# Output product of a hybrid layer: for two of four column groups, rows 8 to 11 move from plain products into the seven block products

## The chip, the cores and the metric

The kernel runs on one core of one Trainium2 chip. The metric is the device time of one execution in microseconds (us), median over runs; lower is better. The core's engines are PE (matrix products; PEld is its weight load), DVE (VectorE), ACT (ScalarE), POOL (GpSimd) and SP (SyncE, which only issues DMAs here).

## The reference

One layer on 512 tokens with 2048 channels. Only the last product is touched by the change.

```python
h = rms_norm(x, norm_g)
z = h @ w_in                                   # 2048 -> 7 x 1024
a_val, a_glu, a_gate, q, k, v, b_gate = split(z)
u = silu(layer_norm(causal_depthwise_conv(a_val * sigmoid(a_glu)), ...))
y_a = (u @ conv_pw_w + conv_pw_b) * silu(a_gate)                  # 1024
y_b = dilated_attention(rms(q), rms(k), v) * silu(b_gate)         # 1024, 16 heads
out = x + concat([y_a, y_b]) @ w_out                              # 2048 x 2048
```

## The kernel before, in words

**Number format.** Every large product is made of fp16 halves: an operand is scaled by a power of two and split into a high part (`A.activation(..., Copy, scale)`, on ACT) and a low part (`V.scalar_tensor_tensor(src, scale, hi, mult, subtract)`, on DVE). One product is then three matmuls (`tri`, L411: high by high L413, high by low L414, low by high L415). The scales come from bounds on the data: squares on ACT, a sum on PE, a reduction and a reciprocal on DVE, a shift and a masking on POOL (`bound`, L193).

**The output product.** The 2048 rows of `w_out` are 16 blocks of 128 rows. The left operand y has the same 16 blocks: 0 to 7 are mixer A ("a"), 8 to 11 are heads 0 to 7 of the attention ("b0"), 12 to 15 heads 8 to 15 ("b1"). The 2048 columns are four column groups g of 512, and the weights come in units of 4 blocks x 512 columns (1 MB; SP issues the load, `wf<-w_dram`). Each column group has

- a unit `("wb", g)`: rows 8 to 11, plain: 4 blocks x 4 token tiles x 3 = 48 matmuls of 128x512. After each token tile DVE adds the bank times a scale into the residual tile: `res<-ps_l,esc,res`, 128x512, four per unit. The scale `esc` is one tiny product on POOL (`evac_scale`, L421).
- three units `("wa", g)`: rows 12 to 15 and rows 0 to 7. Rows 0 to 7 are done as a 2x2 block product with seven products instead of eight (Winograd's form): p1, u, x, p7, p6, p5, z. For them both operands are cut in blocks (weights a11 ... a22, y b11 ... b22) and summed (weights s1 to s4, y t1 to t4). Weight sums s2, s3, s4 are accumulating DMAs that POOL issues (`wf<-wf`), s1 is a subtraction on DVE. Each part then has its high part on ACT and its low part on DVE (`ws<-wf,ws`, 128x1024). In groups 1 to 3 rows 12 to 15 join as a second, smaller set of seven ("c": weights `wsc`, 128x512); in group 0 they are plain, since their y is the last to be ready.

The y parts are `y<-...` on DVE (their low parts): 128x256 for a block, 128x512 for a plain row.

**The order of the work.** It is written out by hand. The program is a sequence of slots, each with 12 matmuls of 128x256 or 6 of 128x512, some 1.3 us. `after(n, fn)` puts a step n slots later, `calendar` by the slot's number. Every engine runs its own queue in program order and waits there for what it needs. The units of the four `wb` run while the last heads are still worked on, and `seven_parts(g)` and `seven_products(g)` give the slots of the weight parts and of the products in each `wa` group, `LENGTH` slots long. `b0` gets its scale `yb0` and its four splits after the fourth pair of heads; the scale `yab` of the other 12 blocks comes when the last head is done, and `y_parts` then makes one y split per slot. Tiles come from small pools: `wide` (8 tiles), `att` (4), `slots`, and `raw` (the fp32 weights), and a load or a split into a tile waits until its last reader is done.

Of the kernel before, what the change touches and what calls it, by code (L numbers as in the profile page):

```python
# [10 lines left out]
F32 = mybir.dt.float32  # L11
# [39 lines left out]
GROUPS += [(kind, g) for kind in ("wb", "wa") for g in range(4)]  # L51
# [34 lines left out]
def layer(ctx: ExitStack, tc: tile.TileContext, xt, w1, w2, w3, g_in, conv_w, conv_b,  # L86
# [156 lines left out]
    for kind, g in GROUPS:  # L243
        if kind == "pw":
            units += [(w2, g, p, kind, g) for p in range(8 // KU)]
        elif kind in OUT_K:
            units += [(w3, g, p, kind, g) for p in OUT_K[kind]]
        else:
            units += [(w1, IN_W1.index((kind, g)), p, kind, g) for p in range(KC // KU)]
# [365 lines left out]
    ob, ysum = {}, {}  # L615
# [6 lines left out]
    def put_y(part, i, y):  # L622

        whole, n, at = ("b0", 4, i) if part == "b0" else ("ab", 12, i + 8 * (part == "b1"))
        if whole not in ysum:
            ysum[whole] = small.tile([P, n], BF16, name=f"ysum{whole}", bufs=1)
        row_squares(y, ysum[whole][:, at:at + 1], S)
        yf[part][i] = y
        if part == "b0" and len(yf[part]) == n:
            def done(s, v):  # L630
                scales["yb0"] = (s, v)
                for k in range(n):
                    after(1 + 2 * k, lambda k=k: y16.update({k + 8: split16(yf["b0"].pop(k), s, "y16")}))
            after(2, lambda: bound("yb0", ysum[whole], done))
        elif part != "b0":
            if part == "a" and i >= 4:
                after(1, lambda: y_sums("", yf["a"], i - 4, i))
            if part == "b1" and i >= 2:
                after(1, lambda: y_sums("c", yf["b1"], i - 2, i))
            if len(yf["a"]) + len(yf["b1"]) == n:  # L640
                after(2, lambda: bound("yab", ysum[whole], y_parts, TOP - 1))
# [4 lines left out]
    def y_sums(c, y, k, below):  # L646

        b11, b12 = (y[k][:, f:f + H] for f in (0, H))
        b21, b22 = (y[below][:, f:f + H] for f in (0, H))
        t12, t34 = slot("ysum"), slot("ysum")  # L650
        t1, t2, t3, t4 = t12[:, :H], t12[:, H:], t34[:, :H], t34[:, H:]
        V.tensor_sub(t1, b11, b12)
        V.tensor_sub(t3, b12, b22)

        def rest():
            V.tensor_add(t2, b22, t1)
            V.tensor_sub(t4, b21, t2)

        after(1, rest)
        for name, t in (("b11", b11), ("b21", b21), ("b22", b22), ("t1", t1), ("t2", t2), ("t3", t3), ("t4", t4)):  # L660
            yt[name + c, k] = t

    def y_parts(s, v):

        scales["yab"] = (s, v)
        place = {}

        def block(name, k):
            with_ = {"b11": "t4", "b21": "t1", "t3": "t2", "t4c": "t3c", "t2c": "t1c"}.get(name)
            if name == "b22":  # L670
                if k % 2 == 0:
                    place["b22", k // 2] = slots.tile([P, 2, 2, H], F16, name="y16", tag="slot")
                t = place["b22", k // 2][:, k % 2]
            elif with_:
                place[with_, k] = slots.tile([P, 2, 2, H], F16, name="y16", tag="slot")
                t = place[with_, k][:, 0]
            else:
                t = place[name, k][:, 1]
            src = yt.pop((name, k))
            tparts[name, k] = (t[:, 0], t[:, 1])  # L680
            A.activation(t[:, 0], src, AF.Copy, scale=s)
            after(1, lambda: V.scalar_tensor_tensor(t[:, 1], src, s, t[:, 0], op0=OP.mult, op1=OP.subtract))

        def plain(k):
            t = slots.tile([P, 2, S], F16, name="y16", tag="slot")
            src = yf["b1"].pop(k)
            y16[12 + k] = (t[:, 0], t[:, 1])
            for b, f in ((1, 0), (2, H)):
                if k >= 2 or b == 1:
                    tparts[f"b{k // 2 + 1}{b}c", k % 2] = (t[:, 0, f:f + H], t[:, 1, f:f + H])  # L690
            A.activation(t[:, 0], src, AF.Copy, scale=s)
            after(1, lambda: V.scalar_tensor_tensor(t[:, 1], src, s, t[:, 0], op0=OP.mult, op1=OP.subtract))

        n = 1
# [155 lines left out]
    def fetch_res(j):  # L850

        if j < 6:
            res[j] = wide_tile("res", [P, 2, S], F32)
        else:
            res[j] = att.tile([P, 2, S], F32, name="res", tag="att")
        nc.sync.dma_start(res[j], rows_of(xt, j))
# [59 lines left out]
    LENGTH = (22, 21, 21, 21)  # L916
# [3 lines left out]
    wparts, plain_w, last, negative = {}, [], [], {}  # L920
    split = [set() for _ in range(4)]

    def seven_parts(g):
# [5 lines left out]
        def block(name):  # L929
            b = PLACE.get(name[:2] if name[0] == "s" else "", name[:3])  # L930
            t = raw[of[0]][:, 2 * (b[2] == "2"):][:, :2] if name[-1] == "c" else raw[of[1 if b[2] == "1" else 2]]
            return t[:, :, H * (b[1] == "2"):][:, :, :H]

        def add(name):

            c = name[2:]
            if name[:2] == "s1":
                V.tensor_tensor(block("a11" + c), block("a22" + c), block("a11" + c), op=OP.subtract)
            elif c and g == 2:
                x, to = SUMS[name[:2]]  # L940
                V.tensor_tensor(block(to + c), block(to + c), block(x + c), op=OP.add)
            else:
                x, to = SUMS[name[:2]]
                nc.gpsimd.dma_start(block(to + c), block(x + c), accum_op=OP.add)
# [3 lines left out]
        def hi(name):  # L948
            if name[-1] == "c":
                t = slots.tile([P, 2, 2, H], F16, name="wsc", tag="slot")  # L950
            else:
                t = part_pool.tile([P, 2, KU, H], F16, name="ws", tag="part")
            wparts[g, name] = t
            A.activation(t[:, 0], block(name), AF.Copy, scale=wscale["wa", g][0])  # L954

        def lo(name):
            t = wparts[g, name]
            V.scalar_tensor_tensor(t[:, 1], block(name), wscale["wa", g][0], t[:, 0], op0=OP.mult, op1=OP.subtract)
            done.add(name)
            if done >= {"s1", "s3"} and of[1] in raw:  # L960
# [3 lines left out]
            if done >= {"s1c", "s2c", "s3c", "s4c"}:  # L964
# [25 lines left out]
        for name, n in begin.items():  # L990
            for c, d in (("", 0), ("c", 1)) if g else (("", 0),):
# [4 lines left out]
    def both_scales(g):  # L996

        if g not in negative:
# [3 lines left out]
            negative[g] = e, ne  # L1002
        return negative[g]

    def seven_products(g):
# [12 lines left out]
        if g == 0:  # L1018
            banks_of.update(v=("22",), z=("12", ("s4", "b22")), u=("21", ("a22", "t4")), x=("11", ("a12", "b21")))
        else:  # L1020
            banks_of = {name: ((w, b), (w + "c", b + "c")) for name, ((w, b),) in banks_of.items()}
# [10 lines left out]
        def product(name, n, m):  # L1032

            what = banks_of[name][n]
            rows = 2 if what[0][-1] == "c" else KU
# [52 lines left out]
        if g == 0:  # L1088
            plan = [(2, alone), (4, lambda: into("22", "v")), (6, lambda: add("11", got["s"])), (12, lambda: into("21", "u")),
                    (14, lambda: (into("11", "x"), store("11"))), (16, lambda: into("22", "p5", ne)),  # L1090
                    (17, lambda: into("12", "p5")), (20, both)]
            order = (("p1", 0), ("v", 0), ("z", 0), ("u", 0), ("x", 0), ("u", 1), ("x", 1), ("p5", 0), ("p7", 0), ("p6", 0), ("z", 1))
            plan += [(2 * n + m, lambda name=name, k=k, m=m: product(name, k, m)) for n, (name, k) in enumerate(order)
                     for m in range(2)]
        else:
            plan = [(3, alone), (6, lambda: into("21", "u")), (7, lambda: add("11", got["s"])),
                    (9, lambda: (into("11", "x"), store("11"))), (15, both), (18, lambda: (into("22", "p5", ne), store("22"))),
                    (18, lambda: into("12", "p5"))]
            for n, name in enumerate(("p1", "u", "x", "p7", "p6", "p5", "z")):
                if (g, name) != (3, "z"):  # L1100
                    plan += [(3 * n + at, lambda name=name, k=k, m=m: product(name, k, m))
                             for at, k, m in ((0, 0, 0), (1, 0, 1), (2, 1, 0), (2, 1, 1))]
# [211 lines left out]

    for i in range(n_plain):
# [34 lines left out]
        else:  # L1350
# [14 lines left out]
            if i + 1 < len(units) and units[i + 1][3] == "wb":  # L1365
                for m in range(2):
                    extra[4 * m].append(lambda m=m: fetch_res(2 * units[i + 1][4] + m))
        if kind == "pw":
# [16 lines left out]
    for g in range(4):  # L1385
        plan = seven_parts(g) + [(n + LENGTH[g], fn) for n, fn in seven_parts(g + 1)] + seven_products(g)
        for n in range(LENGTH[g]):
            clock[0] = BEGIN[g] + n
            if n == 15 and g < 3:
# [55 lines left out]
```

## Time and profile before

| | |
|---|---|
| median of 3 runs | 815.13 us (815.05 to 815.55) |
| profiled execution | 815.08 us |
| its span in the trace | 813.3 us |
| instructions in the span | 13452 |

The span is the time between the first and the last instruction in the trace. The profile gives each engine's busy time and, in "waits", what ended each idle stretch of an engine that had work left. A row of the timeline has the start, the duration, the engine, the source line, the operation, output and inputs, partitions x elements, and in brackets the idle time just before with the instruction that ended it. A matmul's duration is longer than the distance from one to the next, since they are pipelined; the distance is what counts. The same holds, by 0.08 us, for DVE instructions that run back to back. The last units begin at these times of the span: `wb` 0 at 654.87 us, `wb` 2 at 677.51, `wa` 0 at 698.26, `wa` 1 at about 727.1.

### The profile page before, as it was taken

What the parts mean: (1) busy time and instruction counts of PE and PEld (TensorE: products, weight loads), DVE (VectorE), ACT (ScalarE), POOL (GpSimd) and SP (SyncE); (2) the same over time, 40 slices, a digit from 0 to 9 for tenths busy, and PEclk for the clock granted to TensorE, in tenths of its full rate; (3) what the DMA queues carried; (4) which work ended last, traced back from release to release, by engine and by line L of the source; (5) the groups of instructions that cost most, each with busy time, mean ns of one, the idle gap of its engine ahead of it and who ended that gap; (6) DMA issues with size and microseconds to landing.
All of it is one profiled execution on the core that took longest, in us unless ns stands there. A gap on an engine that the chain in (4) does not pass through costs nothing.

```text
span 813.3 us, 13452 instructions
## 1 busy us (share of the span) xinstructions
PE 806.7 (99%) x5271; PEld 500.9 (62%) x5271; DVE 703.3 (86%) x1188; ACT 557.5 (69%) x784; POOL 132.2 (16%) x143
## 2 busy tenths in 40 slices
PE   9999999999999999999999999999999999999998
PEld 6887745888646854444444444444444444788887
DVE  6768999878989989999999989997678798998885
ACT  6667687577756688586757658497688858766540
POOL 0001021322224300004012010000110002412420
PEclk9999999999999999999999999999999999999999
DMA  9852346983874863527474623526352487678752
GB/s 339 329 235 99 109 102 138 142 249 58 311 146 104 149 263 108 122 95 169 142 182 127 150 100 107 123 95 169 104 121 100 137 246 226 118 176 187 130 105 65
DMA packets 98367, 125.60 MB, mean 154 GB/s; under 512 B 62464, under 2 KB 83712, under 8 KB 89088
## 3 DMA queue, kind: packets, MB, share of 16 engines
q1 hardware_dynamic: 80544, 107.37, 42.2%
q0 software_dynamic: 17472, 17.30, 15.0%
q8 instruction: 41, 0.67, 0.3%
q14 instruction: 22, 0.18, 0.1%
q10 hardware_dynamic: 288, 0.07, 0.0%
HBM read 88.56 MB, written 4.19 MB: 114 GB/s over the span
## 4 chain that ended last, share of the span: by engine, by line
PE 90%; DVE 7%; ACT 1%; issue 1%; POOL 0%; DMA 0%; SPq 0%; ACTq 0%; DVEq 0%
PE ps_l L413 24%; PE ps_l L415 23%; PE ps_l L414 23%; PE ps_l L887 10%; DVE cv L81 3%; PE ps_s L413 2%; PE ps_s L415 2%; PE ps_s L414 2%; PE ps_s L730 2%; PE ps_o L771 2%; DVE wl L81 1%; DVE ws L81 1%; ACT junk L191 0%; DVE sx L81 0%; DMA x<-xt_dram 0%
## 5 line engine op out<-in xcount | busy, mean ns | idle before, releaser
L81 DVE SCALAR_TENSOR_TENSOR cv<-u,cw,cv 128x511 f32<-128x511 f32 (+14 forms) x240 | 162.1, 727 | 0.4 <-ACT cv L551 0.4
L191 ACT ACTIVATE junk<-wf 128x2048 uint8<-128x2048 f32 x68 | 129.1, 1899 | 2.4 <-DMA wf<-w_dram 2.1
L300 ACT ACTIVATE wh<-wf,ws 128x2048 f16<-128x2048 f32 x44 | 87.7, 1994 | 52.4 <-PE ps_l L414 50.6
L413 PE MATMUL ps_l<-x,wh 128*128 128x512 f16 x320 | 121.3, 379 | 0.3 <-DVE glu L81 0.3
L415 PE MATMUL ps_l<-x,wl 128*128 128x512 f16 x320 | 121.3, 379 | 0.0
L414 PE MATMUL ps_l<-x,wh 128*128 128x512 f16 x320 | 121.3, 379 | 0.0
L81 DVE SCALAR_TENSOR_TENSOR wl<-wf,ws,wh 128x2048 f16<-128x2048 f32 x45 | 105.6, 2346 | 10.7 <-ACT wh L300 10.7
L413 PE MATMUL ps_l<-wh,x 128*128 128x512 f16 x256 | 97.1, 379 | 0.0
L415 PE MATMUL ps_l<-wh,x 128*128 128x512 f16 x256 | 97.0, 379 | 0.0
L414 PE MATMUL ps_l<-wl,x 128*128 128x512 f16 x256 | 97.0, 379 | 0.0
L81 DVE SCALAR_TENSOR_TENSOR ws<-wf,ws 128x1024 f16<-128x1024 f32 x70 | 89.0, 1278 | 7.1 <-ACT ws L1138 4.5
L413 PEld LDWEIGHTS <-wh 128*128 128x128 f16 x480 | 47.0, 98 | 55.3 <-issue 4.0
L415 PEld LDWEIGHTS <-wl 128*128 128x128 f16 x480 | 46.9, 98 | 53.6 <-DVE wl L81 0.4
L414 PEld LDWEIGHTS <-wh 128*128 128x128 f16 x480 | 46.9, 98 | 50.4 <-issue 0.7
L887 PE MATMUL ps_l<-xr,wr 128*128 128x512 f32 x288 | 69.6, 397 | 0.7 <-ACT xr L338 0.7
L205 POOL TENSOR_SCALAR ws<-ws 128x1 f32<-128x1 f32 x22 | 11.8, 537 | 324.4 <-DVE ws L81 295.6
L887 PEld LDWEIGHTS ps_l<-xr,wr 128*128 128x128 f32 x288 | 53.8, 188 | 14.3 <-ACT xr L338 1.5
L413 PEld LDWEIGHTS <-x 128*128 128x128 f16 x352 | 34.4, 98 | 32.5 <-issue 1.9
L415 PEld LDWEIGHTS <-x 128*128 128x128 f16 x352 | 34.4, 98 | 31.3
L414 PEld LDWEIGHTS <-x 128*128 128x128 f16 x352 | 34.4, 98 | 30.1
L954 ACT ACTIVATE ws<-wf,ws 128x1024 f16<-128x1024 f32 x28 | 32.1, 1147 | 28.3 <-PE ps_l L415 9.7
L1138 ACT ACTIVATE ws<-wf,ws 128x1024 f16<-128x1024 f32 x42 | 47.1, 1138 | 5.8 <-PE ps_l L415 4.8
(251 smaller groups left out, 1816.3 us busy)
## 6 DMA issues: line engine op xcount, KB each, us to landing
wf<-w_dram SPq DMA_DIRECT2D x72, 1024.0 KB, 5.2
wf<-wf POOLq DMA_DIRECT2D x30, 512.0 KB, 6.5
x<-xt_dram SPq DMA_DIRECT2D x16, 256.0 KB, 6.7
res<-xt_dram SPq DMA_DIRECT2D x8, 512.0 KB, 6.6
out_dram<-res SPq DMA_DIRECT2D x15, 256.0 KB, 2.2
wf<-w_dram SPq DMA_DIRECT2D x7, 512.0 KB, 7.2
wf<-wf POOLq DMA_DIRECT2D x6, 256.0 KB, 6.3
wf<-w_dram SPq DMA_DIRECT2D x2, 256.0 KB, 3.1
```

Source lines behind the costliest of these rows:

```text
L81: return getattr(self.engine, name)(out, src, *args, **kw)
L191: A.activation(junk[:, :n], src, AF.Square, scale=scale, accum_out=acc)
L205: G.tensor_scalar(scale, scale, 1e-30, 2.0 ** (-2 * top), op0=OP.max, op1=OP.mult)
L300: A.activation(parts[i][0], raw[i], AF.Copy, scale=wscale[units[i][3:]][0])
L413: T.matmul(ps, ah, bh, start=first, stop=False, skip_group_check=more)
L414: T.matmul(ps, ah, bl, start=False, stop=False, skip_group_check=more)
L415: T.matmul(ps, al, bh, start=False, stop=last, skip_group_check=more)
L730: T.matmul(ps[i, a], qk["q", hf][p4 // 2][rows, p4 % 2, q, i * P:w], qk["k", hf][p4 // 2][rows, p4 % 2, k, :w], start=n == 0, stop=n == 2)
L771: T.matmul(po[rows, i * P:(i + 1) * P], vs[hf][j // 2][:, j % 2, 2 * p4 + a, vp * DH:(vp + 1) * DH], got["t", a][:, pp * (ALL // P) + FROM ...
L887: T.matmul(banks[group, m], wt[:, a, m * P:(m + 1) * P], xk[b], start=k == 0 and a == b == 0, stop=k == KC - 1 and a == 1)
L954: A.activation(t[:, 0], block(name), AF.Copy, scale=wscale["wa", g][0])
L1138: A.activation(t[:, 0], block(name, pair), AF.Copy, scale=wscale[group][0])
```

## The change

For groups g in `JOINED = (0, 1)` the unit `wb` is gone. Its rows 8 to 11 join the seven products as a third set "d": each of the seven products gets 12 more matmuls of 128x256 into a bank that is open anyway (84 per group instead of 48 of 128x512), and four DVE additions per group fall away. For them

- the y of rows 8 to 11 gets block sums (8 additions) and 8 t parts "t1d" to "t4d" (`b0_parts`, in the `pw` units, with the four plain splits that stood behind the fourth pair of heads);
- each joined group gets seven weight parts "d" (`wsd`, 128x512, high on ACT and low on DVE), one more subtraction (s1d) on DVE, three more accumulating DMAs on POOL (s2d, s3d, s4d, 256 KB each) and a scale `wjs` (two tiny products on POOL);
- `y_parts` issues its splits four in three slots, `1 + n * 3 // 4`, instead of one per slot;
- the residual tiles of groups 0 and 1 are fetched later, and the plans of both groups are written anew (`LENGTH` 29 and 28 slots instead of 22 and 21).

```diff
+JOINED = (0, 1)
+GROUPS += [("wb", g) for g in range(4) if g not in JOINED] + [("wa", g) for g in range(4)]
...
+            units += [(w3, g, p, kind, g) for p in OUT_K[kind] + (2,) * (kind == "wa" and g in JOINED)]
...
-            def done(s, v):
-                scales["yb0"] = (s, v)
-                for k in range(n):
-                    after(1 + 2 * k, lambda k=k: y16.update({k + 8: split16(yf["b0"].pop(k), s, "y16")}))
-            after(2, lambda: bound("yb0", ysum[whole], done))
+            after(2, lambda: bound("yb0", ysum[0][:, :4], lambda s, v: scales.update(yb0=(s, v)), TOP - 1))
...
+    def b0_parts():
+        y = yf["b0"]
+        s = scales["yb0"][0]
+        for k in range(4):
+            after(2 * k, lambda k=k: plain("b0", k, s))
+        for k in range(2):
+            after(6 + 3 * k, lambda k=k: y_sums("d", y, k, k + 2))
+            for n in range(4):
+                after(21 + 2 * (2 * n + k), lambda name=f"t{n + 1}d", k=k: block(name, k, s))
...
     def y_parts(s, v):
         scales["yab"] = (s, v)
+        both_scales(0)
+        n = 0
         for name in ("b11", None, "t4", "b21", "t1", "t3", "t2", "b22", "t4c", "t3c", "t2c", "t1c"):
             for k in range(2 if name and name[-1] == "c" else 4):
-                after(n, lambda name=name, k=k: block(name, k) if name else plain(k))
+                after(1 + n * 3 // 4, lambda name=name, k=k: block(name, k, s) if name else plain("b1", k, s))
                 n += 1
...
-    LENGTH = (22, 21, 21, 21)
+    LENGTH = [29, 28, 21, 21]
...
+            elif name[-1] == "d":
+                near = (g, name) in ((0, "a11d"), (0, "a22d"))
+                t = (wide if near else att).tile([P, 2, 2, H], F16, name="wsd", tag="wide" if near else "att")
...
         if g == 0:
-            adds = [(3, "s1", add), (4, "s4", add), (-2, "s2", add), (-8, "s3", add)]
-            begin = {"a11": -6, "a22": -4, "a12": 0, "s1": 5, "s3": 8, "s2": 12, "s4": 16}
+            adds = [(-8, "s3", add), (-2, "s2", add), (3, "s1", add), (4, "s4", add),
+                    (-7, "s3d", add), (5, "s2d", add), (10, "s1d", add), (13, "s4d", add)]
+            begin = {"a11": -6, "a11d": -4, "a22": -3, "a22d": 4, "a12": 0, "s1": 6, "a12d": 11, "s3": 12, "s1d": 14, "s2": 15,
+                     "s3d": 18, "s4": 20, "s2d": 21, "s4d": 24}
...
+            if g in JOINED:
+                t = joined_scale[g] = small.tile([P, 1], F32, name="wjs", bufs=2)
+                G.tensor_tensor(t, wscale["wa", g][0], scales["yab"][0], op=OP.mult)
+                G.tensor_tensor(t, t, scales["yb0"][1], op=OP.mult)
...
+            for name, k in (("p1", 0), ("p1", 1), ("v", 0), ("z", 0), ("u", 0), ("x", 0), ("u", 1), ("u", 2), ("x", 1), ("x", 2),
+                            ("p5", 0), ("p5", 1), ("p7", 0), ("p7", 1), ("p6", 0), ("p6", 1), ("z", 1), ("z", 2)):
...
+    calendar.setdefault(8 * of_group["pw", 0][0] + 6, []).append(b0_parts)
```

Three queues show how the work moves. First POOL, from the scale `yab` on (`yabs`): `esc<-wi,yabi` is the scale of group 0, `nesc` its negative, `esc<-wi,yb0i` that of a `wb` unit, and the DMAs are the accumulations s3, s3d and s2 of group 0. In the kernel before:

```order
L205 TENSOR_SCALAR yabs<-yabs 128x1
L169 TENSOR_TENSOR yabs<-yabs,half 128x1
L426 TENSOR_TENSOR esc<-wi,yb0i 128x1
L205 TENSOR_SCALAR ws<-ws 128x1
L169 TENSOR_TENSOR ws<-ws,half 128x1
L426 TENSOR_TENSOR esc<-wi,yb0i 128x1
L944 DMA wf<-wf 128x4x256
L426 TENSOR_TENSOR esc<-wi,yb0i 128x1
L944 DMA wf<-wf 128x4x256
L426 TENSOR_TENSOR esc<-wi,yabi 128x1
L1001 TENSOR_SCALAR nesc<-esc 128x1
```

and in the changed one:

```order
L206 TENSOR_SCALAR yabs<-yabs 128x1
L170 TENSOR_TENSOR yabs<-yabs,half 128x1
L427 TENSOR_TENSOR esc<-wi,yabi 128x1
L1031 TENSOR_SCALAR nesc<-esc 128x1
L1035 TENSOR_TENSOR wjs<-ws,yabs 128x1
L1036 TENSOR_TENSOR wjs<-wjs,yb0i 128x1
L960 DMA wf<-wf 128x4x256
L960 DMA wf<-wf 128x2x256
L427 TENSOR_TENSOR esc<-wi,yb0i 128x1
L960 DMA wf<-wf 128x4x256
```

The last `esc` of a `wb` unit (unit 3) now stands behind the scales of group 0 and two DMAs, all of which stand behind `yabs`.

Second DVE, from the reciprocal of `yab` on. `res` is the addition of a finished bank, `wl` the low part of a plain weight unit, `y_...<-ag` and `y_...<-ysum` low parts of y blocks, `y_...<-gate` of 128x512 those of plain rows. Before:

```order
L81 RECIPROCAL yabi<-yabs 128x1
L81 SCALAR_TENSOR_TENSOR res<-ps_l,esc,res 128x512
L81 SCALAR_TENSOR_TENSOR y_6749<-ag_5132,yabs,y_6749 128x256
L81 SCALAR_TENSOR_TENSOR wl<-wf,ws,wh 128x2048
L81 SCALAR_TENSOR_TENSOR y_6760<-ag_5132,yabs,y_6760 128x256
L81 SCALAR_TENSOR_TENSOR res<-ps_l,esc,res 128x512
L81 SCALAR_TENSOR_TENSOR y_6774<-ag_5173,yabs,y_6774 128x256
L81 SCALAR_TENSOR_TENSOR y_6784<-ag_5173,yabs,y_6784 128x256
```

and after the change:

```order
L82 RECIPROCAL yabi<-yabs 128x1
L82 SCALAR_TENSOR_TENSOR y_6512<-ysum,yb0s,y_6512 128x256
L82 SCALAR_TENSOR_TENSOR res<-ps_l,esc,res 128x512
L82 SCALAR_TENSOR_TENSOR y_6540<-ysum,yb0s,y_6540 128x256
L82 SCALAR_TENSOR_TENSOR y_6765<-ag_5125,yabs,y_6765 128x256
L82 SCALAR_TENSOR_TENSOR y_6767<-ag_5125,yabs,y_6767 128x256
L82 SCALAR_TENSOR_TENSOR wl<-wf,ws,wh 128x2048
L82 SCALAR_TENSOR_TENSOR y_6779<-ag_5165,yabs,y_6779 128x256
L82 SCALAR_TENSOR_TENSOR ws<-wf,ws 128x1024
L82 SCALAR_TENSOR_TENSOR res<-ps_l,esc,res 128x512
L82 SCALAR_TENSOR_TENSOR y_6797<-ag_5165,yabs,y_6797 128x256
```

The addition `res` that follows the reciprocal belonged to unit `wb` 1 of four; it is now the first of unit 3, the last plain one, and the first weight part `ws` of group 0 (a11) stands eight instructions behind the reciprocal instead of 34.

Third DVE again, within the work of group 0, in the changed kernel alone (`wsd` is new): `wsd` is the low part of a joined weight part, here a22d, and `wf<-wf` the subtraction s1.

```order
L82 TENSOR_TENSOR wf<-wf 128x4x256
L82 SCALAR_TENSOR_TENSOR y_6917<-gate,yabs,y_6917 128x256
L82 SCALAR_TENSOR_TENSOR y_6941<-gate,yabs,y_6941 128x256
L82 SCALAR_TENSOR_TENSOR wsd<-wf,wjs,wsd 128x512
L82 SCALAR_TENSOR_TENSOR res<-ps_l,esc,res 128x2x256
L82 SCALAR_TENSOR_TENSOR y_6900<-ysum,yabs,y_6900 128x256
```

These stand in one queue with the y splits, and all of them come between the reciprocal and the last products of group 0.

More of the change, by code (lines that the diff above doesn't have):

```diff
@@ L639, in put_y @@
                 after(1, lambda: y_sums("c", yf["b1"], i - 2, i))
-            if len(yf["a"]) + len(yf["b1"]) == n:
-                after(2, lambda: bound("yab", ysum[whole], y_parts, TOP - 1))
+            if len(yf["a"]) + len(yf["b1"]) == 12:
+                after(2, lambda: bound("yab", ysum[0], y_parts, TOP - 1))
     yt, tparts = {}, {}
@@ L660, in y_sums, with block @@
         for name, t in (("b11", b11), ("b21", b21), ("b22", b22), ("t1", t1), ("t2", t2), ("t3", t3), ("t4", t4)):
-            yt[name + c, k] = t
+            if name[0] == "t" or not c:
+                yt[name + c, k] = t
+    place = {}
+    def block(name, k, s):
+        with_ = {"b11": "t4", "b21": "t1", "t3": "t2", "t4c": "t3c", "t2c": "t1c"}.get(name)
+        if name == "b22":
+            if k % 2 == 0:
+                place["b22", k // 2] = slots.tile([P, 2, 2, H], F16, name="y16", tag="slot")
+            t = place["b22", k // 2][:, k % 2]
+        elif name[-1] == "d":
+            if ("d", k) not in place:
+                place["d", k] = att.tile([P, 4, 2, H], F16, name="y16", tag="att")
+            t = place["d", k][:, int(name[1]) - 1]
+        elif with_:
+            place[with_, k] = slots.tile([P, 2, 2, H], F16, name="y16", tag="slot")
+            t = place[with_, k][:, 0]
+        else:
+            t = place[name, k][:, 1]
+        src = yt.pop((name, k))
+        tparts[name, k] = (t[:, 0], t[:, 1])
+        A.activation(t[:, 0], src, AF.Copy, scale=s)
+        after(1, lambda: V.scalar_tensor_tensor(t[:, 1], src, s, t[:, 0], op0=OP.mult, op1=OP.subtract))
@@ new lines, in plain @@
+    def plain(part, k, s):
+        t = slots.tile([P, 2, S], F16, name="y16", tag="slot")
+        src = yf[part][k]
+        if part == "b1":
+            yf[part].pop(k)
+        c, at = ("c", 12) if part == "b1" else ("d", 8)
+        y16[at + k] = (t[:, 0], t[:, 1])
+        for b, f in ((1, 0), (2, H)):
+            if k >= 2 or b == 1:
+                tparts[f"b{k // 2 + 1}{b}{c}", k % 2] = (t[:, 0, f:f + H], t[:, 1, f:f + H])
+        A.activation(t[:, 0], src, AF.Copy, scale=s)
+        after(1, lambda: V.scalar_tensor_tensor(t[:, 1], src, s, t[:, 0], op0=OP.mult, op1=OP.subtract))
@@ L684, in plain @@
[L684 to L692, printed above, removed]
@@ L850, in fetch_res @@
     def fetch_res(j):
[L852 to L855, printed above, removed]
+        res[j] = wide_tile("res", [P, 2, S], F32)
         nc.sync.dma_start(res[j], rows_of(xt, j))
@@ L953, in hi, with scale_of @@
             wparts[g, name] = t
-            A.activation(t[:, 0], block(name), AF.Copy, scale=wscale["wa", g][0])
+            A.activation(t[:, 0], block(name), AF.Copy, scale=scale_of(name))
+        def scale_of(name):
+            return joined_scale[g] if name[-1] == "d" else wscale["wa", g][0]
         def lo(name):
             t = wparts[g, name]
-            V.scalar_tensor_tensor(t[:, 1], block(name), wscale["wa", g][0], t[:, 0], op0=OP.mult, op1=OP.subtract)
+            V.scalar_tensor_tensor(t[:, 1], block(name), scale_of(name), t[:, 0], op0=OP.mult, op1=OP.subtract)
             done.add(name)
+            if done >= {"s1d", "s2d", "s3d", "s4d"} and g in JOINED and of[3] in raw:
+                free(of[3])
             if done >= {"s1", "s3"} and of[1] in raw:
@@ L1034, in product @@
             what = banks_of[name][n]
-            rows = 2 if what[0][-1] == "c" else KU
+            rows = 2 if what[0][-1] in "cd" else KU
             for to, tokens in spot(name, m):
@@ new lines, in seven_products @@
+            n = 0
+            for name, k in (("p1", 0), ("p1", 1), ("v", 0), ("z", 0), ("u", 0), ("x", 0), ("u", 1), ("u", 2), ("x", 1), ("x", 2),
+                            ("p5", 0), ("p5", 1), ("p7", 0), ("p7", 1), ("p6", 0), ("p6", 1), ("z", 1), ("z", 2)):
+                joined = banks_of[name][k][0][-1] == "d"
+                plan += [(n + m * (not joined), lambda name=name, k=k, m=m: product(name, k, m)) for m in range(2)]
+                n += 1 if joined else 2
+        else:
+            w = LENGTH[g] // 7
+            plan = [(w, alone), (2 * w, lambda: into("21", "u")), (2 * w + 1, lambda: add("11", got["s"])),
+                    (3 * w, lambda: (into("11", "x"), store("11"))), (5 * w, both),
+                    (6 * w, lambda: (into("22", "p5", ne), store("22"))), (6 * w, lambda: into("12", "p5"))]
```

76 lines of the change are left out of this document (33 added, 43 removed).

## The prediction

> **What bounds the kernel now.** I read the page first: busy shares, the slices, the chain that ended last.
>
> ```profile
> PE 806.7 (99%) x5271; PEld 500.9 (62%) x5271; DVE 703.3 (86%) x1188; ACT 557.5 (69%) x784; POOL 132.2 (16%) x143
> PEclk9999999999999999999999999999999999999999
> ```
>
> PE is busy 99% of the span of 813.3 us, at full clock in every slice. Whatever shortens PE's work shortens the kernel, as long as the others keep up. DVE, at 86%, has the least room of them. Next the waits of PE, all of which come to 3 us; two matter here:
>
> ```profile
> PE ps_s L147 <- POOL wz L144: 1.0, 1, 1.0
> PE ps_s L575 <- DVE lnacc L81: 1.0, 1, 1.0
> ```
>
> Then the windows around the change. Columns: PE busy, PEld, DVE, ACT, POOL (instructions), granted clock, DMA share, GB/s.
>
> ```profile
> 623.80:634.10 10.30, 10.30 (x49) 4.67 (x48) 10.13 (x26) 9.93 (x19) 0.00 (x0) 1.00 0.47 155
> 634.10:644.50 10.40, 10.40 (x50) 4.70 (x49) 6.47 (x11) 10.40 (x22) 0.00 (x0) 1.00 0.17 54
> 644.50:654.90 10.40, 10.40 (x51) 4.73 (x50) 9.07 (x18) 5.09 (x7) 1.08 (x4) 1.00 1.02 250
> 654.90:669.20 14.30, 14.30 (x120) 7.29 (x119) 13.79 (x28) 8.37 (x13) 0.94 (x3) 1.00 0.70 234
> 669.20:698.30 29.10, 29.10 (x138) 13.17 (x136) 25.49 (x39) 22.63 (x35) 4.84 (x5) 1.00 0.68 217
> 698.30:727.10 28.80, 28.80 (x266) 25.81 (x265) 25.76 (x44) 21.46 (x32) 11.77 (x12) 1.00 0.69 148
> ```
>
> The first four are the `pw` units and the first plain output units, the fifth the rest of the plain units, the sixth group 0 of the block products. In the last two PE never stops, and DVE works 51.3 of 57.9 us. So PE is the bound, and DVE's queue is 11% away from it in the very stretch to which the change adds DVE work. That is what the forecast turns on.
>
> **What the change takes from PE.** The distance between matmuls, from the first and last of 78 of 128x512 and of 94 of 128x256:
>
> ```profile
> 499.86 0.38 PE L413 MATMUL ps_l<-x,wh 128*128 128x512 f16 x1
> ...
> 516.48 0.38 PE L415 MATMUL ps_l<-x,wl 128*128 128x512 f16 x1
> 716.73 0.27 PE L414 MATMUL ps_l<-y,ws 128*128 128x256 f16 x1
> ...
> 726.89 0.27 PE L414 MATMUL ps_s<-y,ws 128*128 128x256 f16 x1
> ```
>
> 16.62 us / 77 = 0.2158 us and 10.16 / 93 = 0.1092 us. A joined group loses 48 x 0.2158 = 10.36 us and gets 84 x 0.1092 = 9.17, a gain of 1.18; two groups give 2.4 us. The new matmuls have the shape and the alternation of weights of the second row pair, so I put no bounds on this.
>
> Four low parts of 128x512 leave DVE's queue from ahead of `lnacc`, at 0.66 us each (rows below) 2.6 us. PE's wait of 1.0 us there should go. Bounds 0, should DVE be late there for something else, and 1.0; I take 1.0. ACT, at 69%, gets 22 small instructions more, and SP two issues; I cost both at nothing, because in the fifth and sixth windows ACT is idle for 13.8 of 57.9 us.
>
> **What it adds to DVE.** The distances of DVE's instructions, with `wl` 128x2048, `ws` 128x1024, `res` and y 128x512, y 128x256, and the forms whose mean is all I have (less 0.08 us of overlap):
>
> ```profile
> 691.81 2.35 DVE L81 SCALAR_TENSOR_TENSOR wl<-wf,ws,wh 128x2048 f16<-128x2048 f32 x1
> 694.07 0.48 DVE L81 SCALAR_TENSOR_TENSOR y<-ysum,yabs,y 128x256 f16<-128x256 f32 x1
> 694.47 1.28 DVE L81 SCALAR_TENSOR_TENSOR ws<-wf,ws 128x1024 f16<-128x1024 f32 x1
> 695.66 0.74 DVE L81 SCALAR_TENSOR_TENSOR res<-ps_l,esc,res 128x512 f32<-128x512 f32 x1
> 696.32 0.87 DVE L81 SCALAR_TENSOR_TENSOR y<-ysum,yabs,y 128x256 f16<-128x256 f32 x2
> 697.11 1.28 DVE L81 SCALAR_TENSOR_TENSOR ws<-wf,ws 128x1024 f16<-128x1024 f32 x1
> 678.38 0.74 DVE L81 SCALAR_TENSOR_TENSOR y<-gate,yabs,y 128x512 f16<-128x512 f32 x1
> 679.04 0.16 DVE L81 TENSOR_REDUCE ws<-ps_s 128x1 f32<-128x3 f32 x1
> L81 DVE SCALAR_TENSOR_TENSOR wsc<-wf,ws,wsc 128x512 f16<-128x512 f32 x21 | 15.6, 743 | 0.0
> L81 DVE TENSOR_TENSOR wf<-wf 128x1024 f32<-128x1024 f32 x10 | 12.2, 1217 | 1.1 <-DMA wf<-wf 1.1
> ```
>
> That is 2.26, 1.20, 0.66, 0.66 and 0.40 us; `wsd` has the form of `wsc`, 0.66; the subtraction 1.14.
>
> Nothing of y blocks 0 to 7 can be split before the scale `yab`, and all of it must be split for the products. So I add up one queue, from the reciprocal of `yab` to the low part of s2d, the weights of the second half of product p6 of group 0. In the changed program 70 DVE instructions stand in between: 37 y of 256 (14.8 us), 7 `ws` (8.4), 6 `wsd` (4.0), 9 `res` (5.9), 4 y of 512 (2.6), one `wl` (2.3), the subtractions s1 (1.1) and s1d (0.6, half the size), a `res` addition (0.6) and three tiny ones (0.2): 40.5 us.
>
> What PE has to do meanwhile: before the products of s2d come 300 matmuls of group 0, 300 x 0.1092 = 32.8 us, and the rest of the plain units ahead. Those two units and the attention pair between them take, from the first to the third unit's start, 677.51 - 654.87 = 22.64 us, as in the trace:
>
> ```profile
> 654.87 0.38 PE L413 MATMUL ps_l<-y,wh 128*128 128x512 f16 x1
> ...
> 677.51 0.38 PE L413 MATMUL ps_l<-y,wh 128*128 128x512 f16 x1
> 669.13 0.17 DVE L81 RECIPROCAL yabi<-yabs 128x1 f32<-128x1 f32 x1
> ```
>
> The reciprocal ended 14.4 us after the first of those starts. At that distance 8.2 us of plain work are left behind it, instead of 698.26 - 669.30 = 29.0 before. The second plain pair is what used to hide the y splits, and its removal is the heart of the loss. The reciprocal also comes later: ahead of it DVE gets 4 y of 512, 8 additions and 6 t parts of 256, 4 x 0.66 + 14 x 0.40, about 8 us. In the first four windows DVE was idle for 45.4 - 39.5 = 5.9 us, so about 2 us stick out. Bounds: nothing (idle time further ahead takes them) and 3.9 (half of them, since idle time lies where something else is awaited). Taken 2.0: PE has 6.2 + 32.8 = 39.0 us of work (bounds 8.2 - 3.9 + 32.8 = 37.1 and 8.2 + 32.8 = 41.0), against DVE's 40.5.
>
> **New waits in that queue.** DVE's second instruction after the reciprocal is the first `res` of plain unit 3, which needs its `esc` from POOL. That now stands behind group 0's `esc`, `nesc`, two `wjs` and two DMAs, all released by the reciprocal. The POOL rows:
>
> ```profile
> 680.56 0.19 POOL L426 TENSOR_TENSOR esc<-wi,yb0i 128x1 f32<-128x1 f32 x1
> 680.73 1.35 POOL L944 DMA_DIRECT2D wf<-wf  x1
> 681.62 2.61 POOL L426 TENSOR_TENSOR esc<-wi,yb0i 128x1 f32<-128x1 f32 x1
> 700.42 2.95 POOL L1001 TENSOR_SCALAR nesc<-esc 128x1 f32<-128x1 f32 x1
> 704.88 3.87 POOL L944 DMA_DIRECT2D wf<-wf  x3 [1.50 <-DMA wf<-wf]
> ```
>
> At the least 4 x 0.19 + 2 x 0.9 (from a DMA's start to the next instruction's) + 0.19 = 2.7 us; at the most 0.19 x 3 + 2.95 + 2 x 1.3 + 0.3 = 6.4. DVE gets there after 0.4, so it waits 2.3 to 6.0 us. I take 4.6: the nearest row is the `esc` behind a DMA, which took 2.61 us instead of 0.19, and here it stands behind two (2.7 - 0.19 + 2.61 - 0.4 = 4.7). Behind the waiting `res` stand all y splits and the first weight part, a11, without which p1 cannot begin: PE's gap shows first there.
>
> The Trainium skill ("SBUF — State Buffer", A bandwidth-pool intuition that's wrong) says that a DMA issued on GpSimd which takes about 620 ns alone takes about 3100 ns beside a VectorE instruction that holds their shared port, since the descriptors can't be written. The slow `esc` row fits that. By that rule DVE's own waiting would free the port, and the wait would be at its lower end: a sum lower by 2.3 us, 817.9.
>
> Two subtractions, s1 and s1d, change the raw weights in place and wait for accumulating DMAs that read them, and those DMAs wait for low parts just ahead in DVE's own queue. Landing times, and the wait of this kind now:
>
> ```profile
> wf<-wf POOLq DMA_DIRECT2D x30, 512.0 KB, 6.5
> wf<-wf POOLq DMA_DIRECT2D x6, 256.0 KB, 6.3
> DVE wf L81 <- DMA wf<-wf: 1.1, 1, 1.1
> ```
>
> 5.1 and 5.3 us of DVE work lie between, so 1.4 and 1.0 are missing: 2.4 us. Bounds: 0, if DVE by then is late for other reasons, and 3.9, with the 1.50 us that the last POOL row waited for its predecessor's data.
>
> Group 1 I cost at nothing. Its window before:
>
> ```profile
> 727.10:754.60 27.50, 27.50 (x254) 24.65 (x252) 24.21 (x32) 18.01 (x21) 7.49 (x8) 1.00 0.80 164
> ```
>
> DVE's 24.2 us get 7 `wsd` and an s1d, 5.2, against 28 slots x 12 x 0.1092 = 36.7 us of PE: 7 us of cover. Were it gone, the same two waits as in group 0 would come again, 2.4 us (in rival 4).
>
> **The sum.** Stall of PE = 40.5 + 4.6 + 2.4 - 39.0 = 8.5 us. Low: 40.5 + 2.3 + 0 - 41.0 = 1.8. High: 40.5 + 6.0 + 3.9 - 37.1 = 13.3. The profiled execution, 815.08, has 1.8 us around its span and stands at the median of 815.13, so I count from 815.1: 815.1 - 2.4 - 1.0 + 8.5 = 820.2 us.
>
> **The rivals.** 0.2% (1.6 us: 813.5 to 816.8) is about what a measurement of this kernel can tell from no change.
>
> 1. *Faster: DVE keeps up.* The one mechanism: the reciprocal comes no later and DVE's waits on POOL and DMA stay at their low ends. Speaking for it: the 5.9 idle us would nearly take the added 8, and POOL is busy 16%. Against it: POOL cannot run ahead, since its row starts with the same scale. It decides at a stall of 1.8 us, just at the low bound: 811.7 to 813.5 us.
> 2. *No change.* A stall of 1.8 to 5.1 us, with one wait of the two at its low end: 813.5 to 816.8; around 815 the 3.4 us of gain are just eaten.
> 3. *A colder PE on top.* The first matmuls of the span, after idle time, go at another pace:
>
> ```profile
> L147 PE MATMUL ps_s<-wz 128*128 128x512 f16 x9 | 3.4, 557 | 1.0 <-POOL wz L144 1.0
> ```
>
> Nine took 3.44 us instead of 8 x 0.2158 + 0.38 = 2.1, so a restart costs 1.3 us. If the gap at p1 brings that on: 821.5 us. The Trainium skill ("TensorE: Matmul & The Clock Gate", Part 1: The HAM clock gate) has TensorE fall to half rate after an idle window of about 3.4 us; by that, one gap of the size of POOL's wait would do it, while several short ones would not. No run here has shown such a gap yet.
> 4. *More waits than I counted* (group 1's parts, raw weight tiles held until s4d and so later loads): beyond 822.5, up to 826.
>
> That the joining does nothing at all is excluded by the two distances.
>
> **Chances.** Stall of 5.1 to 10.7 us without a colder PE (816.8 to 822): 0.48; colder PE 0.15; further waits 0.10; no change 0.15; faster 0.12. Faster by over 0.2%: 0.12; within: 0.15; slower: 0.73. The low end leaves out the faster case, 813.6; the high one most of the further waits, 824.6. The likeliest case has 816.8 to 822.
>
> **What would show it.** Right: in the changed trace PE's waits have rows on DVE (`ws`, `y` or `wsd`) of 5 us or more in group 0, first at p1; DVE has a wait of 3 us or more of `res` on POOL's `esc`, and one or two of `wf` on `wf<-wf`; DVE is busy or so waiting throughout group 0; the wait on `lnacc` is gone; the new matmuls lie 0.109 us apart. Wrong: PE's waits stay near 2 us (then DVE's lead was longer than I counted), or the `esc` wait is absent and the loss sits on a load or on ACT, or the granted clock falls below full in group 0 (rival 3).

## The result: 5.5 us slower, and the profile after

The changed kernel takes 820.83 us (median of 4 runs, 820.59 to 821.17), the kernel before 815.3 us in the same comparison: a ratio of 1.0068, 95% interval 1.0051 to 1.0086. The profiled execution took 820.97 us, its span is 819.0 us, 5.7 us more than before. The forecast was 820.2 us, in the range 813.6 to 824.6.

The page of the changed kernel first: busy times, the granted clock in 40 slices, and the chain that ended last.

```profile
PE 807.8 (99%) x5341; PEld 509.8 (62%) x5341; DVE 709.3 (87%) x1204; ACT 564.2 (69%) x804; POOL 135.7 (17%) x147
PEclk9999999999999999999999999999999998999999
PE 91%; DVE 5%; DMA 1%; ACT 1%; issue 1%; POOL 1%; SPq 0%; ACTq 0%; POOLq 0%; DVEq 0%
```

PE has less work and yet 1 us more busy time, and the granted clock has an 8 in the slice from 676 to 696 us. The waits of PE (engine, line, engine waited for: us in total, times, longest):

```profile
PE ps_l L416 <- DVE ws L82: 4.0, 1, 4.0
PE ps_s L204 <- ACT junk L192: 1.9, 1, 1.9
PE ps_s L148 <- POOL wz L145: 1.0, 1, 1.0
PE ps_l L415 <- DVE y L82: 0.5, 1, 0.5
```

`lnacc` is gone from the list; three new rows have 6.4 us. The timeline of POOL behind the scale `yab`:

```profile
673.20 0.29 POOL L427 TENSOR_TENSOR esc<-wi,yabi 128x1 f32<-128x1 f32 x1 [0.53 <-DVE yabi L82]
674.02 0.19 POOL L1036 TENSOR_TENSOR wjs<-wjs,yb0i 128x1 f32<-128x1 f32 x1
674.65 2.58 POOL L960 DMA_DIRECT2D wf<-wf  x2 [0.43 <-issue]
676.25 1.20 POOL L427 TENSOR_TENSOR esc<-wi,yb0i 128x1 f32<-128x1 f32 x1
```

and that of DVE, which waits for the last of these:

```profile
672.89 0.16 DVE L82 RECIPROCAL yabi<-yabs 128x1 f32<-128x1 f32 x1
672.97 0.47 DVE L82 SCALAR_TENSOR_TENSOR y<-ysum,yb0s,y 128x256 f16<-128x256 f32 x1
677.48 0.75 DVE L82 SCALAR_TENSOR_TENSOR res<-ps_l,esc,res 128x512 f32<-128x512 f32 x1 [4.04 <-POOL esc L427]
```

DVE stood still from 673.44 to 677.48 us, with all y splits and the first weight part behind it. PE, in the timeline of the first products of group 0 and of p6 (p1 starts at 678.34):

```profile
678.34 0.27 PE L414 MATMUL ps_l<-y,ws 128*128 128x256 f16 x1
679.07 0.27 PE L415 MATMUL ps_l<-y,ws 128*128 128x256 f16 x1 [0.46 <-DVE y L82]
683.33 0.39 PE L416 MATMUL ps_l<-y,ws 128*128 128x256 f16 x1 [3.99 <-DVE ws L82]
683.51 0.42 PE L414 MATMUL ps_l<-y,ws 128*128 128x256 f16 x1
...
688.87 0.39 PE L415 MATMUL ps_l<-y,wsd 128*128 128x256 f16 x1
689.09 0.29 PE L416 MATMUL ps_l<-y,wsd 128*128 128x256 f16 x1
689.21 0.27 PE L414 MATMUL ps_l<-y,wsd 128*128 128x256 f16 x1
...
689.87 0.27 PE L414 MATMUL ps_l<-y,wh 128*128 128x256 f16 x1
...
718.68 0.27 PE L414 MATMUL ps_l<-y,wsd 128*128 128x256 f16 x1
```

After the gap the matmuls go 0.22 us apart until 689.09, then 0.11. The 34 matmuls of 128x256 from 683.33 to 689.87 took 6.54 us instead of 34 x 0.1092 = 3.71; less 0.08 for a small one among them, the cold clock (the stretch in which the granted clock was half) cost 2.75 us. The windows show the same (columns as in the prediction: PE, PEld, DVE, ACT, POOL, granted clock, DMA share, GB/s):

```profile
672.90:684.00 11.10, 6.66 (x32) 3.04 (x31) 7.06 (x11) 11.10 (x18) 3.65 (x7) 0.92 0.82 180
684.00:700.00 16.00, 16.00 (x126) 13.38 (x125) 15.28 (x28) 9.10 (x17) 5.68 (x5) 0.84 0.62 142
700.00:716.00 16.00, 16.00 (x149) 14.34 (x148) 16.00 (x31) 14.04 (x26) 8.56 (x8) 1.00 0.73 159
716.00:728.00 12.00, 12.00 (x113) 10.75 (x111) 11.96 (x18) 8.78 (x12) 2.40 (x2) 1.00 1.12 315
```

PE is "busy" for all 16 us of the second window, but with 126 matmuls instead of 149. DVE is busy for 43.2 of the 44 us from 684 to 728. Near the end of that queue stands the low part of s2d:

```profile
717.80 0.75 DVE L82 SCALAR_TENSOR_TENSOR wsd<-wf,wjs,wsd 128x512 f16<-128x512 f32 x1
```

It ends at 718.55, and PE takes it up at 718.68 without a wait: 0.13 us to spare. So the account of the 5.7 us is: joining -2.4, `lnacc` -1.2 (the last attention pair but one starts at 610.99 instead of 612.23), PE's wait at the sum for `yab` +1.9, the gaps at p1 +0.46 and +3.99, the cold clock +2.75: +5.5.

### The profile page after: what moved, and what is told of

The parts are those of the page before. It is cut to its first block, busy times and chain, and to the rows that moved or that the text cites. A ratio compares the mean times of both kernels' runs of the same rounds, so it can differ in the third digit from the quotient of the medians.

```text
span 819.0 us, 13637 instructions
## 1 busy us (share of the span) xinstructions
PE 807.8 (99%) x5341; PEld 509.8 (62%) x5341; DVE 709.3 (87%) x1204; ACT 564.2 (69%) x804; POOL 135.7 (17%) x147
## 4 chain that ended last, share of the span: by engine, by line
PE 91%; DVE 5%; DMA 1%; ACT 1%; issue 1%; POOL 1%; SPq 0%; ACTq 0%; POOLq 0%; DVEq 0%
PE ps_l L414 24%; PE ps_l L416 23%; PE ps_l L415 23%; PE ps_l L900 10%; PE ps_s L414 2%; PE ps_s L416 2%; PE ps_s L415 2%; PE ps_s L746 2%; PE ps_o L787 2%; DVE ws L82 1%; DMA pt<-hl 1%; ACT junk L192 1%; DVE wl L82 1%; DVE ysum L82 0%; DVE y L82 0%
## 5 line engine op out<-in xcount | busy, mean ns | idle before, releaser
L301 ACT ACTIVATE wh<-wf,ws 128x2048 f16<-128x2048 f32 x42 | 83.8, 1994 | 53.3 <-PE ps_l L415 51.4
L82 DVE SCALAR_TENSOR_TENSOR wl<-wf,ws,wh 128x2048 f16<-128x2048 f32 x43 | 100.9, 2347 | 10.7 <-ACT wh L301 10.7
L414 PEld LDWEIGHTS <-wh 128*128 128x128 f16 x448 | 43.9, 98 | 53.5 <-issue 6.2
L416 PEld LDWEIGHTS <-wl 128*128 128x128 f16 x448 | 43.8, 98 | 49.9 <-DVE wl L82 0.7
L415 PEld LDWEIGHTS <-wh 128*128 128x128 f16 x448 | 43.8, 98 | 47.1 <-issue 0.8
L206 POOL TENSOR_SCALAR ws<-ws 128x1 f32<-128x1 f32 x20 | 9.1, 457 | 307.8 <-DVE ws L82 307.4
L1178 ACT ACTIVATE ws<-wf,ws 128x1024 f16<-128x1024 f32 x42 | 47.1, 1138 | 5.7 <-PE ps_l L416 4.8
L170 POOL TENSOR_TENSOR ss<-ss,half 128x8 f32<-128x8 f32 x16 | 31.4, 1969 | 116.8 <-DVE ss L82 116.7
```

The costliest lines, as they stand in the source:

```text
L82: return getattr(self.engine, name)(out, src, *args, **kw)
L170: G.tensor_tensor(ap, ap, half.to_broadcast(list(ap.shape)), op=OP.pow)
L206: G.tensor_scalar(scale, scale, 1e-30, 2.0 ** (-2 * top), op0=OP.max, op1=OP.mult)
L301: A.activation(parts[i][0], raw[i], AF.Copy, scale=wscale[units[i][3:]][0])
L414: T.matmul(ps, ah, bh, start=first, stop=False, skip_group_check=more)
L415: T.matmul(ps, ah, bl, start=False, stop=False, skip_group_check=more)
```

## The experiments

Two theories were open. By the *queue theory* group 0 cannot end before DVE's queue from `yab` on, and the gap at p1 and the cold clock are only the places where PE's lag shows. By the *gap theory* these two are the loss itself, and without them DVE keeps up. All ratios below are against the kernel before, on the same chip (its medians there: 815.03 us in the first four runs, 815.22 in the last four).

**Esc first.** POOL computes the scale of plain unit 3 at the head of the scales.

```diff
 def y_parts(s, v):
     scales["yab"] = (s, v)
+    for w in range(4):
+        if w not in JOINED:
+            evac_scale(("wb", w))
     both_scales(0)
```

> The changed kernel, but POOL computes the scale esc of plain unit 3 ahead of group 0's scales and DMAs. Queue theory (the loss is the length of DVE's queue from the reciprocal of yab to s2d; PE's gap at p1 and its cold clock are only where the lag shows): DVE's wait of 4.0 us on esc goes, its queue becomes 40.5 + 0.6 = 41.1 us against 5.3 + 32.8 = 38.1 us of PE work, a lag of 3.0 us in place of the gaps 0.5 + 4.0 and the 2.75 us of cold clock: 820.8 - 4.2 = 816.6 us (815.9 to 817.4), with PE waits on later parts of group 0. Gap theory (the gap at p1 and the cold clock behind it are the loss, DVE otherwise keeps up): 820.8 - 4.0 - 2.75 = 814.1 us (813.5 to 814.8), no PE wait above 0.5 us behind p1.

Measured: 816.31 us (815.8 to 816.88), ratio 1.0013 (1.0005 to 1.0022). DVE's wait on `esc` is gone, and this is PE's list from 676 us on:

```profile
PE ps_l L415 <- DVE y L82: 0.8, 1, 0.8
PE ps_l L416 <- DVE wsd L82: 0.7, 1, 0.7
PE ps_l L416 <- DVE ws L82: 0.5, 1, 0.5
```

The clock is full in every window. The 7.2 us of gaps and cold clock are gone, and 2.0 us of waits stand in their place, most of them on later parts; the last one, 0.65 us at 713.70, is on s2d, the end of the queue. That is 5.2 us between the two profiled executions (spans of 819.0 and 813.8) and 4.5 between the medians. The queue theory's 816.6 holds, the gap theory's 814.1 does not.

**The gap filled.** Matmuls of zeros keep PE going while it waits for p1.

```diff
 first, last_ = ...
+if (g, name, n, m) == (0, "p1", 0, 0):
+    for _ in range(40):
+        T.matmul(to, wz, wz[:, None, :].to_broadcast([P, 2, P]), start=True, stop=True)
```

> The changed kernel with 40 matmuls of zeros (128x256, some 4.4 us) on PE ahead of p1 of group 0, which fill the gap in which PE waits, so that the clock should stay full. Queue theory: the time stays at 820.8 us (820.3 to 821.3); what the clock no longer costs comes back as PE waits on wsd or ws of group 0. Gap theory: the 2.75 us of cold clock are saved, 818.1 us (817.5 to 818.7).

Measured: 820.95 us, ratio 1.0071 (1.0059 to 1.0084), the same as the changed kernel. The clock stayed full, and the waits came back elsewhere. First the window that had 0.84, then PE's waits in group 0:

```profile
684.00:700.00 16.00, 15.12 (x137) 13.03 (x136) 15.27 (x28) 9.04 (x17) 5.68 (x5) 1.00 0.62 141
```

```profile
PE ps_l L416 <- DVE wsd L82: 1.0, 2, 0.7
PE ps_l L415 <- DVE y L82: 0.8, 1, 0.8
PE ps_s L416 <- DVE wsd L82: 0.5, 1, 0.5
```

The last of these waits, 0.65 us at 719.76, is on s2d again. This is the clearest of the runs: a clock loss of 2.75 us was real and cost nothing, since PE was slowed while it would have had to wait for DVE anyway. The four executions of the changed kernel agree: their granted clock over the span was 0.996 in the profiled one and 0.998 in the others, which by an estimate (0.002 of 819 us) is 1.6 us less of lost clock, and their times lie within 0.6 us.

**Less on DVE.** Esc first, and the low parts of group 0's joined weights left out.

```diff
-V.scalar_tensor_tensor(t[:, 1], block(name), scale_of(name), t[:, 0], ...)
+if g or name[-1] != "d":
+    V.scalar_tensor_tensor(t[:, 1], block(name), scale_of(name), t[:, 0], ...)
```

> As the run with esc first, but the low parts of the seven joined weight parts of group 0 are left out (the products take the high part twice), 7 x 0.66 = 4.6 us less on DVE, PE's work the same. Queue theory: the queue is 41.1 - 4.0 = 37.1 us against 38.1, no lag left: 813.6 us (812.9 to 814.3), 3 us below the run with esc first. Gap theory: the same as that run within 0.5 us, near 814.1.

Measured: 814.11 us (813.76 to 814.7), ratio 0.9988 (0.9980 to 0.9997), 2.2 us under esc first where the queue theory said 3 and the gap theory none. (That the time is the gap theory's 814.1 is chance: it had expected that already of esc first.) What is left of PE's waits in the plain units and group 0 is 1.9 us for the sum of `yab`, 0.5 and 0.4 at p1 and a plain row. The waits on `wsd` are gone, and from p1 on there are 0.9 us instead of 2.0. That is as much as the two profiled executions differ by (spans of 812.7 and 813.8); the other 1.1 us between the medians the traces do not show. A shorter queue on DVE paid, then, with PE's work the same.

**The splits alone.** The kernel before, with only the four y splits of rows 8 to 11 moved.

```diff
-after(1 + 2 * k, lambda k=k: y16.update({k + 8: split16(yf["b0"].pop(k), s, "y16")}))
+calendar.setdefault(8 * of_group["pw", 0][0] + 6, []).append(b0_parts)   # the same four, 2 slots apart
```

> The kernel before with one part of the change alone: the four splits of y rows 8 to 11 go from behind the fourth pair of heads into the pw units; nothing joins. If PE's wait of 1.0 us on lnacc was due to them: 814.3 us (814.0 to 814.6). If another wait takes its place, or the later scale yab costs something: 815.3 us within 0.4.

Measured: 814.83 us, ratio 0.9997 (0.9988 to 1.0005): no change that can be told, a little under the second expectation and over the first. The wait on `lnacc` did go, and the last attention pair but one starts 1.3 us earlier (610.94 against 612.23). But the first plain unit starts at 654.00 against 654.87, and the block products at 697.82 against 698.26. 0.3 us of that is a new wait of PE:

```profile
PE ps_l L415 <- DVE wl L81: 0.3, 1, 0.3
```

Where the rest went the trace does not name. In these two executions a gain of 1.3 us that is there at 611 us is 0.4 us at the end.

**T parts later.** Esc first, and the t parts of rows 8 to 11 behind the last gates.

```diff
-after(21 + 2 * (2 * n + k), lambda name=f"t{n + 1}d", k=k: block(name, k, s))
+after(36 + 2 * (2 * n + k), lambda name=f"t{n + 1}d", k=k: block(name, k, s))
```

> As the run with esc first (816.3 us), but the eight t parts of rows 8 to 11 are split 15 slots later, behind the last gates and the sum for yab. Theory that these parts (and their waits on ACT) hold up the last gate, so that PE waits 1.7 to 1.9 us for ACT's last row squares: that PE wait goes, the scale yab comes earlier, while 3.2 us of DVE work move behind it: 815.4 us (814.6 to 816.3). Rival, that PE only arrives there earlier because the wait on lnacc is gone: the wait stays at 1 us or more and the longer queue costs: 817 to 819 us.

Measured: 814.11 us (813.09 to 814.72), ratio 0.9985 (0.9976 to 0.9993), better than either expectation. PE's wait for ACT at the sum of `yab` is gone, and the reciprocal starts at 667.53 instead of 672.12 us. So the t parts did hold up the chain of gates and row squares on DVE and ACT. Six of the eight had stood ahead of the reciprocal, 2.4 us of DVE work, yet the scale came 4.6 us earlier: in esc first DVE had also waited 0.45, 0.93 and 1.15 us for their high parts on ACT, and none of these waits is left. The changed kernel has the same waits, and its trace shows what two of them hang on:

```profile
655.99 0.51 ACT L680 ACTIVATE y<-ysum,yb0s 128x256 f16<-128x256 f32 x1 [1.25 <-DMA pt<-hl]
656.53 0.48 DVE L82 SCALAR_TENSOR_TENSOR y<-ysum,yb0s,y 128x256 f16<-128x256 f32 x1 [1.22 <-ACT y L680]
```

The t parts get their two tiles from the pool `att`, which also holds `hl`, the split probabilities of the attention. ACT could write the first part into each tile only when SP's transposing DMA had read `hl` (it had waited 2.67 us for the tile before this one), and DVE stood behind ACT with the gates behind it. Issued 9 or 15 slots later, the parts find their tiles free: in the three runs in that order ACT starts them without such a wait. No run gives the parts another pool, so how much of the 4.6 us is the tiles and how much the parts' own work is read from these rows and not shown apart. One late t part now makes PE wait 0.87 us at 694.85, in group 0.

**One split per slot.** Esc first, with the spacing of before.

```diff
-after(1 + n * 3 // 4, lambda name=name, k=k: ...)
+after(1 + n, lambda name=name, k=k: ...)
```

> As the run with esc first (816.3 us), but the y splits go one per slot as before the change, not four in three slots. Queue theory: ten of the 256-wide low parts (10 x 0.40 = 4.0 us) fall behind s2d in DVE's queue, more than its lag of 3.0 us; what then decides are the last blocks b22 of y, about as late as PE: 814.3 us (813.6 to 815.0), with small PE waits on y rows. Rival, that the denser spacing is needed since y would come late for the products: 816.3 us or more, with PE waits on y of 3 us or more.

Measured: 815.61 us (815.24 to 816.64), ratio 1.0005 (0.9996 to 1.0014): 0.7 us better than esc first by the medians, with intervals that overlap, and not the 2.0 expected. The waits on `ws` and `wsd` in group 0 went, but others took their place, four on y:

```profile
PE ps_l L415 <- DVE y L82: 1.8, 4, 0.8
```

These are one at p1 and three at the plain rows 12 to 15, whose splits come later by this spacing. So the denser spacing is not needed for the blocks, and it does help those rows. The rival's 3 us of waits did not come either.

**One group.** Group 1 alone is joined.

```diff
-JOINED = (0, 1)
+JOINED = (1,)
-LENGTH = [29, 28, 21, 21]
+LENGTH = [22, 28, 21, 21]
+# group 0: plan, order of products and fetch of the residual as before, begin {"a11": -8, "a22": -4, "a12": -1, "s1": 4, "s3": 7, "s2": 11, "s4": 14}
+# esc first; t parts at 30 instead of 21; "d" parts at +4 instead of +6
```

> Only group 1 is joined; group 0 as before the change with its weight parts begun one or two slots earlier, three plain units stay ahead of it, esc first, t parts 9 slots later, the d parts of group 1 two slots earlier. Queue theory: a third plain unit gives PE 12 us more work behind the scale yab and DVE's queue loses six wsd, so no lag: 815.1 - 1.2 (one joined group) - 1.3 (lnacc) + 0.4 (a wait on wl, as in the run with the splits moved alone) = 813.0 us (812.3 to 813.8). Rival, that a joined group does not pay by itself: 814.8 us or more.

Measured: 813.38 us (813.06 to 813.69), ratio 0.9976 (0.9966 to 0.9986). It is as the queue theory expected. In this order the three plain units are cover enough: from p1 on PE waits for nothing that its list shows. A wait of 0.9 us on `wl` came in place of `lnacc`.

**Two groups, in another order.** Both joined, as in the change.

```diff
+# esc first
-after(21 + 2 * (2 * n + k), ...)          # t parts
+after(30 + 2 * (2 * n + k), ...)
-after(1 + n * 3 // 4, ...)                # y splits
+after(1 + n, ...)
-(("", 0), ("c", 1), ("d", 6))             # group 1's parts
+(("", 0), ("c", 1), ("d", 4))
```

> Both groups joined as in the change, with esc first, one y split per slot, t parts 9 slots later and the d parts of group 1 two slots earlier. Queue theory: DVE's work ahead of s2d falls by 4.0 us and no wait on POOL is left, so that the 2.4 us of the joining and the 1.3 us of lnacc show but for some 2 us of PE waits on plain y rows and the last y blocks: 813.4 us (812.5 to 814.4). Rival, that two plain units cannot cover DVE's queue in any order: 815.5 us or more.

Measured: 812.32 us (812.18 to 813.0), ratio 0.9964 (0.9951 to 0.9976). It is a little under the expected range. This beats both kernels, by 2.9 us the one before and by 8.5 the changed one, with the same work on every engine and only its order changed. Its busy times on the page, and the longest entry of PE's waits:

```profile
PE 804.4 (99%) x5341; PEld 508.2 (63%) x5341; DVE 709.1 (87%) x1204; ACT 564.1 (70%) x804; POOL 132.9 (16%) x147
```

```profile
PE ps_l L415 <- DVE y L82: 1.1, 2, 0.6
```

PE's waits are back at 2.9 us in sum, near the 3.2 of before, so most of the 2.9 us of gain is the joining itself. The forecast 2 us of waits on plain rows and the last y blocks came to 1.1.

## Why the prediction was right

The loss was forecast where it arose, in DVE's queue behind the scale, and most of the signs came true: DVE's wait on `esc` (4.0 us, 3 or more forecast), one wait of `wf` on `wf<-wf`, no `lnacc`, first gap at p1, 0.11 us between the new matmuls. PE's rows on DVE in group 0 came to 4.5 us, not to 5, with the cold clock in place of the rest; and two signs of being wrong were there as well, the clock below full and a part of the loss on ACT.

- *The joining, -2.4.* The new matmuls go 0.11 us apart at full clock. The re-ordered kernel shows the gain when DVE does not stand in the way.
- *`lnacc`, -1.0.* Measured -1.2 up to 611 us. Alone, in the run with only the splits moved, two thirds were given back; the forecast took the wait's removal for a gain at the end, which this run did not show.
- *DVE's queue, 47.5 us with its waits.* From the reciprocal's end (673.05) to the end of s2d's turn (718.46) it took 45.4: 40.8 of work (40.5 forecast), 4.0 on `esc` (4.6 forecast), 0.6 on the first subtraction and none on the second (2.4 forecast). That last term was mis-sized: the two subtractions began 5.6 and 4.7 us after the issue of the DMAs ahead of them (689.24 and 697.90), and the forecast had taken the median landings of 6.5 and 6.3.
- *PE's work beside it, 39.0.* Measured 678.34 - 673.05 = 5.3 of plain work and 32.8, 38.1. Lag 45.4 - 38.1 = 7.3, forecast 8.5; the gaps at p1 and the cold clock add up to 0.46 + 3.99 + 2.75 = 7.2. They could have been less, with waits on later parts for the rest, as in the runs with esc first and with the gap filled; that they use up the lag almost to the end is chance.
- *ACT at nothing, and the scale 2.0 us later.* This step failed. The reciprocal ended 19.4 us after the first plain unit's start (673.05 - 653.62) instead of 14.4, so it came 5.0 us later, beyond the bound of 3.9. The DVE work that the forecast counted ahead of it was there, but not the waits for ACT on the t parts, 2.7 us in three rows, two of which hang on the tiles of `att`. They put the last gate and its row squares late, and PE waited 1.9 us at the sum for `yab`, in a place the forecast did not name. That ACT has idle time in the two windows behind does not bear on this: the waits lie at 652 to 665 us. With the 1.9 the stall is 9.1 us; 815.1 - 2.4 - 1.2 + 9.1 = 820.6. That the 820.2 came out so near is luck: 1.2 us too much in the lag of group 0 and 1.9 us forgotten here nearly cancelled.
- *Rival 3, the colder PE.* It happened, at 2.75 us, twice the 1.3 estimated from the warm-up row. Added to the 820.2, as the rival did, it would have given too much: it ran inside the lag. By the rule of the Trainium skill ("TensorE: Matmul & The Clock Gate", Part 1: The HAM clock gate) one gap of about 3.4 us brings half rate, and the trace agrees in kind: after the gap of 3.99 us the distance was 0.22 us instead of 0.11, and the next longest wait in these traces, 1.95 us at the sum for `yab`, did not do that. The granted clock was already down to 0.50 in the gap's last us (682.3 to 683.3), some 2.9 us after its start, sooner than by that rule.
- *The port rule* ("SBUF — State Buffer" of the Trainium skill, A bandwidth-pool intuition that's wrong) would have put the wait on `esc` at 2.3 us. It was 4.0, though DVE was idle. The `esc` started 1.6 us after the first of the two DMAs, less than the 1.8 counted, but it took 1.20 us instead of 0.19, and from the reciprocal's end to the first DMA 1.6 us went by where 0.8 was counted. The row of 2.58 us covers both DMAs, which overlap, and in the run with esc first, where DVE was busy throughout, it is 2.58 us too. So nothing here shows that DVE's state mattered to them.

## What to carry to other kernels

Where an engine off the bound has all of its work behind one late scale, add up its queue from that scale to each use and compare it with the work that the bound has meanwhile: that difference, not the sum of the visible gaps, is the loss behind the scale. Taking away work that hid such a queue (here two of four plain units, 20 us of PE) can cost more than the work itself saved, as it did here until the order was made anew for it. A tiny instruction of one engine on which a busy engine's queue waits belongs ahead of everything on its queue that it does not need. And work that is moved ahead of a chain can wait for a buffer as well as for an engine: see what released its first instruction.

## What the runs showed that was not expected

A gap of 4.0 us on PE was followed by 5.8 us at half pace (0.22 instead of 0.11 us from 683.33 to 689.09), and filling it with matmuls of zeros kept the clock at 1.00 and saved nothing. And the small t parts, of which 2.4 us of DVE work stood ahead of the scale, delayed it by 4.6 us: the rest is DVE's waiting for ACT, which for its part had twice waited for a tile that the attention still held.
